# Filter features first, output sums in SBUF with 512-column products, and stores in a second DMA queue: a hybrid encoder layer

## The chip, the cores and the metric

One core of a Trainium2 chip runs the whole layer. The metric is the device time of one execution in microseconds (us); lower is better. Engines are named as in the profile: PE is TensorE (matmuls; PEld its weight loads), DVE is VectorE, ACT is ScalarE, POOL is GpSimd, SP is SyncE, which here only issues DMAs. HBM is the memory off the core, SBUF the memory on it, PSUM the banks that PE writes its sums to.

## What is computed

One layer, applied to two sequences of their own: p with 1024 tokens and s with 512, both of width 1024.

```
h = rmsnorm(x); z = h @ w_in                       # w_in is 1024 x 4096
x0, x1, vv = short_conv(first 3*512 columns of z)
y_hy  = x0 * long_conv(x1 * vv, hyena_filter(L))   # FFT convolution, filter from a small sine MLP
y_hy  = rmsnorm(y_hy) * silu(hy_gate)
q, k, v = att_qkv; q, k = rmsnorm(q), rmsnorm(k)   # 8 heads of 64
y_att = rmsnorm(neighbourhood_attention(q, k, v)) * silu(att_gate)
out = x + concat(y_hy, y_att) @ w_out              # w_out is 1024 x 1024
hyena_filter: h = sin(fr1*(z@w1 + b1)); h = sin(fr2*(h@w2 + b2)); h @ w3, times a decay
```

## The kernel before

Every large product is split into a high and a low part of each factor (`hi`, `lo`, type fp32r) and takes three matmuls: hi·hi, lo·hi, hi·lo. The weights come as 128x1024 tiles (`wraw`); ACT or DVE rounds each half to `whi` (line 364), POOL subtracts to get `wlo` (line 365), and `take_w` hands them out in the order of a list that `plan` has written ahead (lines 320 to 330).

The work is a sequence of stages. In each, `weave` (line 332) alternates between generators by a table of spans and priorities (`run`, lines 1133 to 1139), and a scheduler then sets the order of the instructions on each engine.

1. **Opening** (lines 1164 to 1173). The x tiles of p are loaded, squared on ACT, scaled on DVE by a reciprocal root (`x_norm`, `rsqrt`: 15 small DVE instructions), transposed on PE, and split into `hThi_p` (ACT) and `hTlo_p` (DVE) (`x_turn`), in two halves (segments) of 512 tokens. Then come the filter features (`filters_mlp`, line 155): two layers, three segments of 512 columns (two of p, one of s), each with one matmul, seven DVE instructions on `arg` and `n` and a sine on ACT.
2. **Filters** (`k_phase`): the filters times the decay (`dec`), their transforms stored to HBM (`K_d`), woven with the projections for q, k, v and gates of p, which are stored to HBM too (`qk_d`, `v_d`, `ga_d`). The tile `vg` of the v projection has one buffer: ACT writes its high part, DVE its low part, four DMAs store it, and only then comes the next.
3. **hyena_p**: convolutions of p, results to HBM (`A_d`).
4. **Attention of p with hyena and projections of s.**
5. **Output with attention of s.** `out_part(part, jobs)`: part 0 multiplies the hyena half, part 1 the attention half. The jobs are three blocks of 512 tokens: p first half (P0), p second half (P1), s. The order is part 0 of P0 and P1, part 1 of both, part 0 of s, and after the attention of s part 1 of s. A product is 128 tokens by 256 columns; two of them fill one PSUM bank. The sums of P0 and s stay in SBUF (`acc`, which starts as x). Those of P1 go through HBM: ACT scales the bank to `oo` (line 1106), `sum<-oo` stores it, and later `oy<-sum` and `ox` are loaded, added on POOL and finished on DVE.

All DMAs, loads and stores alike, are issued by SP in one in-order queue (`dma`, line 58):

```
def dma(self, out, in_):
    eng = (self.nc.sync, self.nc.scalar)[0]
    eng.dma_start(out=out, in_=in_)
```

Of the kernel before, what the change touches and what calls it, by code (L numbers as in the profile page):

```python
# [38 lines left out]
class Group:  # L39
    def __init__(self, name, L, x, out, z2, dec, tw0):  # L40
        self.name, self.L, self.x, self.out, self.z2, self.dec = name, L, x, out, z2, dec
        self.nt = L // P
# [4 lines left out]
        self.nseg = L // 512


class Kernel:  # L50
# [49 lines left out]
    def setup(self):  # L100
# [48 lines left out]
    def mlp_load(self):  # L149
        for w, nm in zip(self.w12, ("w1", "w2")):  # L150
            self.dma(w, self.io[nm])
        for G in (self.P_, self.S_):
            self.dma(self.z[G.name], G.z2)

    def filters_mlp(self, G, mp):
        nc = self.nc
        w1, w2 = self.w12
        h = self.z[G.name]
        for layer, (w, b, fr) in enumerate(((w1, "b1", "fr1"), (w2, "b2", "fr2"))):
            nxt = None if layer else mp.tile([P, G.L], F32, name=f"h1_{G.name}")  # L160
            for s in range(G.nseg):
                sl = slice(s * 512, (s + 1) * 512)
                ps = self.bank("ml")
                nc.tensor.matmul(ps, lhsT=w, rhs=h[:, sl], start=True, stop=True)
                arg = mp.tile([P, 512], F32, name="arg", bufs=2)
                self.ts(arg, ps, self.v[b], ALU.add, self.v[fr], ALU.mult)
                n = mp.tile([P, 512], F32, name="n", bufs=2)
                magic = 12582912.0
                self.ts(n, arg, 1.0 / TWO_PI, ALU.mult, magic, ALU.add)
                self.ts(n, n, magic, ALU.subtract)  # L170
                c1 = 6.28125
                c2 = 0.0019350051879882812
                c3 = TWO_PI - c1 - c2
                self.stt(arg, n, -c1, arg)
                self.stt(arg, n, -c2, arg)
                self.stt(arg, n, -c3, arg)
                self.ts(arg, arg, 3.1415925, ALU.min, -3.1415925, ALU.max)
                nc.scalar.activation(out=nxt[:, sl] if nxt else arg, in_=arg, func=AF.Sin)
                if layer:
                    self.stack([t[:, sl] for t in self.hm[G.name]], arg)  # L180
            h = nxt
            yield
# [35 lines left out]
    def x_norm(self, G, xp, ahead):  # L218

        nc = self.nc  # L220
        G.xs = []
        for s in range(G.nseg):
            ss = xp.tile([P, 4], F32, name="ss", bufs=2)
            for j in range(4):
                tt = s * 4 + j
                x = xp.tile([P, D], F32, name="x", bufs=G.nt)
                self.dma(x, G.x[tt * P:(tt + 1) * P, :])
                sq = xp.tile([P, D], F32, name="xsq", bufs=1)
                nc.scalar.activation(out=sq, in_=x, func=AF.Square, accum_out=ss[:, j:j + 1])
                G.xs.append(x)  # L230
                if ahead:
                    ahead.pop(0)()
            r = self.rsqrt(xp, ss, 4, 1.0 / D, "x")
            for j in range(4):
                x = G.xs[s * 4 + j]
                self.ts(x, x, r[:, j:j + 1])

    def x_turn(self, G, hps):

        nc = self.nc  # L240
        G.hi = [p.tile([P, KC, 512], F32R, name=f"hThi_{G.name}") for p in hps]
        G.lo = [p.tile([P, KC, 512], F32R, name=f"hTlo_{G.name}") for p in hps]
        for s in range(G.nseg):
            for k in range(KC):
                ps = self.bank()
                for j in range(4):
                    nc.tensor.transpose(out=ps[:, j * P:(j + 1) * P], in_=G.xs[s * 4 + j][:, k * P:(k + 1) * P], identity=self.ident)
                gk = self.v["norm_g"][:, k:k + 1]
                nc.scalar.activation(out=G.hi[s][:, k], in_=ps, func=AF.Copy, scale=gk)
                self.stt(G.lo[s][:, k], ps, gk, f32(G.hi[s][:, k]), ALU.subtract)  # L250
# [43 lines left out]
    def steps(self, what):  # L294
# [1090 lines left out]
```

## Time and profile before

| | |
|---|---|
| median of 3 runs | 1091.8 us (1089.95 to 1094.8) |
| the profiled execution: time, span | 1090.92 us, 1089.1 us |
| PE, DVE, ACT, POOL busy | 92%, 73%, 43%, 38% |
| granted TensorE clock, mean | 0.982 |
| DMA: one queue of program transfers | 153.69 MB |

The span runs from the first to the last instruction. The profiled execution lies 0.9 us under the median. PE's busy share counts modelled ends of pipelined matmuls, and time at the lower clock as busy, so it overstates what PE achieved.

### The profile page before, as it was taken

The numbers are of one execution on the slowest core, as the hardware profiler recorded it, in microseconds if no ns is written. First come the engines' busy times: TensorE is split into PE (matmuls) and PEld (weight loads), VectorE is DVE, ScalarE is ACT, GpSimd is POOL, SyncE is SP. The second block draws the span as 40 slices with busy tenths as digits, with TensorE's granted clock in tenths as the row PEclk, the third lists the DMA queues.
The fourth block names the chain that finished last, engine by engine and source line by source line (L and its number), as shares of the span: only waits on it lengthen the run. The fifth ranks groups of instructions, "written<-read, shape, count | busy, mean of one in ns | idle before, by whom it ended". The sixth has DMA issues, their size and how long they took to land.

```text
span 1089.1 us, 18072 instructions
## 1 busy us (share of the span) xinstructions
PE 1003.6 (92%) x6444; PEld 906.6 (83%) x6444; DVE 800.1 (73%) x2134; ACT 463.1 (43%) x958; POOL 415.5 (38%) x336
## 2 busy tenths in 40 slices
PE   3898999988999999999989999987989989899997
PEld 2698999977788888888877887876968879899987
DVE  5997779552157767967559999887967977587874
ACT  6453334233331323122124565655747653476530
POOL 2032332112142323123256344354254356784651
PEclk9999999999999999999989999999999999999999
DMA  8226372756312121212483354435544478966522
GB/s 299 69 78 195 119 235 91 242 161 241 109 39 80 58 62 58 67 54 92 173 240 106 94 145 130 129 100 168 141 133 115 132 237 263 295 183 211 173 72 97
DMA packets 112216, 154.84 MB, mean 142 GB/s; under 512 B 7953, under 2 KB 80475, under 8 KB 111615
## 3 DMA queue, kind: packets, MB, share of 16 engines
q1 hardware_dynamic: 112127, 153.69, 45.3%
q8 instruction: 51, 0.84, 0.3%
q14 instruction: 38, 0.31, 0.1%
HBM read 110.35 MB, written 43.32 MB: 141 GB/s over the span
## 4 chain that ended last, share of the span: by engine, by line
PE 48%; DVE 27%; DMA 12%; issue 5%; ACT 4%; SPq 2%; POOL 1%; POOLq 0%; DVEq 0%; ACTq 0%
PE bank L391 25%; PE bank L1094 7%; PE bank L443 3%; PE bank L404 3%; DMA dec<-in_dec_p_dram 2%; PE bank L1012 2%; SPq L60 2%; DVE zc L63 2%; DMA v_p<-vg 2%; DMA v_s<-vg 2%; PE bank L445 2%; PE bank L444 2%; DVE s_sb L981 2%; PE bank L1003 2%; DVE s L63 1%
## 5 line engine op out<-in xcount | busy, mean ns | idle before, releaser
L365 POOL TENSOR_TENSOR wlo<-wraw,whi 128x512 fp32r<-128x512 f32 x160 | 233.7, 1464 | 514.3 <-ACT whi L364 322.5
L391 PE MATMUL bank<-hThi_p,whi 128*128 128x512 f32 x320 | 126.8, 396 | 3.9 <-DVE vg L63 3.2
L391 PE MATMUL bank<-hThi_p,wlo 128*128 128x512 f32 x320 | 126.7, 396 | 0.0
L391 PE MATMUL bank<-hTlo_p,whi 128*128 128x512 f32 x320 | 126.3, 395 | 0.0
L404 PE MATMUL bank<-whi,hThi_p 128*128 128x256 f32 x384 | 111.6, 293 | 6.3 <-DVE vg L63 3.2
L1094 PE MATMUL bank<-whi,hi 128*128 128x256 f32 x384 | 111.6, 292 | 6.0 <-ACT oo L1106 2.6
L1094 PE MATMUL bank<-whi,lo 128*128 128x256 f32 x384 | 110.7, 292 | 0.9 <-POOL lo L63 0.9
L1094 PE MATMUL bank<-wlo,hi 128*128 128x256 f32 x384 | 110.9, 290 | 0.0
L404 PE MATMUL bank<-wlo,hThi_p 128*128 128x256 f32 x384 | 110.6, 289 | 0.0
L404 PE MATMUL bank<-whi,hTlo_p 128*128 128x256 f32 x384 | 108.4, 287 | 0.0
L985 ACT ACTIVATE s_sb<-s_sb,mx 128x360 f32<-128x360 f32 (+1 forms) x96 | 60.3, 629 | 88.2 <-DVE mx L981 87.8
L364 ACT CAST whi<-wraw 128x512 fp32r<-128x512 f32 x66 | 40.9, 623 | 108.0 <-PE bank L391 72.9
L1094 PEld LDWEIGHTS bank<-whi,hi 128*128 128x128 f32 x384 | 75.4, 196 | 7.4 <-ACT oo L1106 2.8
L404 PEld LDWEIGHTS bank<-whi,hThi_p 128*128 128x128 f32 x384 | 74.2, 194 | 8.2 <-DVE vg L63 3.7
L364 DVE CAST whi<-wraw 128x512 fp32r<-128x512 f32 x94 | 58.6, 626 | 27.6 <-POOL lo L63 6.8
L1094 PEld LDWEIGHTS bank<-whi,lo 128*128 128x128 f32 x384 | 74.6, 196 | 1.6 <-POOL lo L63 1.6
L404 PEld LDWEIGHTS bank<-wlo,hThi_p 128*128 128x128 f32 x384 | 74.5, 194 | 1.0 <-issue 1.0
L1094 PEld LDWEIGHTS bank<-wlo,hi 128*128 128x128 f32 x384 | 75.2, 196 | 0.0
L391 PEld LDWEIGHTS bank<-hThi_p,whi 128*128 128x128 f32 x320 | 60.4, 189 | 17.1 <-DVE vg L63 4.1
L404 PEld LDWEIGHTS bank<-whi,hTlo_p 128*128 128x128 f32 x384 | 73.3, 193 | 0.3 <-issue 0.2
L391 PE MATMUL bank<-hThi_s,whi 128*128 128x512 f32 x160 | 65.6, 413 | 8.4 <-DVE vg L63 4.9
L1012 PE MATMUL bank<-pt,V 120*64 120x256 f32 (+1 forms) x352 | 66.5, 295 | 6.6 <-DVE pt L63 4.2
(279 smaller groups left out, 2765.8 us busy)
## 6 DMA issues: line engine op xcount, KB each, us to landing
wraw<-in_w_ch_dram SPq DMA_DIRECT2D x40, 512.0 KB
wraw<-in_w_tk_dram SPq DMA_DIRECT2D x24, 512.0 KB
wraw<-in_w_out_dram SPq DMA_DIRECT2D x16, 512.0 KB
V<-v_p SPq DMA_DIRECT2D x32, 240.0 KB
v_p<-vg SPq DMA_DIRECT2D x32, 160.0 KB
K_p<-Kw SPq DMA_DIRECT2D x4, 1088.0 KB
x<-in_x_prompt_dram SPq DMA_DIRECT2D x8, 512.0 KB
dec<-in_dec_p_dram SPq DMA_DIRECT2D x16, 256.0 KB
```

The costliest lines, as they stand in the source:

```text
L60: eng.dma_start(out=out, in_=in_)
L63: (eng or self.nc.vector).tensor_tensor(out=out, in0=a, in1=b, op=op)
L364: next(self.w_round)(out=hi, in_=r)
L365: nc.gpsimd.tensor_tensor(out=lo, in0=r, in1=f32(hi), op=ALU.subtract)
L391: nc.tensor.matmul(ps, lhsT=w, rhs=h[s][:, k], start=(k == 0 and i == 0), stop=(k == KC - 1 and i == 2))
L404: nc.tensor.matmul(pss[t // 2][:, t % 2, :], lhsT=h[t // 4][:, k, t % 4 * P:(t % 4 + 1) * P], rhs=w, start=(k == 0 and i == 0 and t % 2 == ...
L443: mm(o, lhsT=c, rhs=z, start=True, stop=False)
L444: mm(o[:, 0:P], lhsT=ns if inverse else s, rhs=z[:, 1], start=False, stop=False)
L445: mm(o[:, P:], lhsT=s if inverse else ns, rhs=z[:, 0], start=False, stop=True)
L985: nc.scalar.activation(out=s_sb[:, :n], in_=s_sb[:, :n], func=AF.Exp, bias=mx, scale=-1.0, accum_out=l)
L1012: nc.tensor.matmul(o, lhsT=vl, rhs=pr_, start=(c == 0 and i == 0), stop=(c == ncu - 1 and i == 1))
L1094: nc.tensor.matmul(ps[:, j, :], lhsT=h[:, tok], rhs=w, start=(k == 0 and i == 0 and j == 0), stop=(k == 3 and i == 2 and j == 1))
```

## The change

The feature layer of the filters is cut into single segments (`mlp_seg`). The first segment of p, with its loads, comes ahead of x, and a hand-set order on DVE covers the opening: segment 0 of layer one, both halves of x, then the rest. One step of the argument reduction is dropped (three multiply-adds become two), and a Newton step of `rsqrt` takes three DVE instructions in place of four. The first two `wlo` are made on DVE. In the output all three jobs keep their sums in SBUF, each product has 512 columns and fills a bank by itself, part 0 runs for all three jobs at once (so w_out is loaded 12 times 512 KB and not 16), and `sum`, `oo`, `oy` and `ox` are gone. All stores are issued by ACT (`store`).

```diff
+    def store(self, out, in_):
+        self.nc.scalar.dma_start(out=out, in_=in_)
...
+        self.w_low = itertools.chain([nc.vector] * 2, itertools.repeat(nc.gpsimd))
...
-    def filters_mlp(self, G, mp):
...
+    def mlp_seg(self, G, mp, layer, s):
...
+        ps = self.bank("ml")
+        nc.tensor.matmul(ps, lhsT=w, rhs=h[:, sl], start=True, stop=True)
+        arg = mp.tile([P, 512], F32, name="arg", bufs=2)
+        self.ts(arg, ps, b, ALU.add, fr, ALU.mult)
+        n = mp.tile([P, 512], F32, name="n", bufs=2)
+        magic = 12582912.0
+        self.ts(n, arg, 1.0 / TWO_PI, ALU.mult, magic, ALU.add)
+        self.ts(n, n, magic, ALU.subtract)
+        c1 = 6.28125
+        self.stt(arg, n, -c1, arg)
+        self.stt(arg, n, c1 - TWO_PI, arg)
+        self.ts(arg, arg, 3.1415925, ALU.min, -3.1415925, ALU.max)
+        nc.scalar.activation(out=arg if layer else self.h1[G.name][:, sl], in_=arg, func=AF.Sin)
...
             self.mul(t, y, y)
-            self.mul(t, t, h)
-            self.ts(t, t, -0.5, ALU.mult, 1.5, ALU.add)
-            self.mul(y, y, t)
+            self.stt(t, t, -0.5, h, ALU.mult)
+            self.stt(y, t, 1.5, y, ALU.mult, ALU.add)
...
-            return [[]] + [[("w_out", g, int(what[3]))] for g in range(4)]
+            n = {"out0": 3, "out1": 2, "out1s": 1}[what]
+            return [[]] + [[("w_out", h, int(what[3]), u) for u in range(2)] if j == 0 else [] for h in range(2) for j in range(n)]
...
-            nc.gpsimd.tensor_tensor(out=lo, in0=r, in1=f32(hi), op=ALU.subtract)
+            self.sub(lo, r, f32(hi), next(self.w_low))
...
-        self.dma(self.K_d[G.name][blk], K)
+        self.store(self.K_d[G.name][blk], K)
...
+        for h in range(2):
+            hs = slice(h * 512, (h + 1) * 512)
+            units = [self.take_w(("w_out", h, part, k // 2)) for k in range(4)]
             for jb in jobs:
...
+                if part == 0:
+                    self.dma(acc[:, :, hs], G.x[t0 * P:(t0 + 4) * P, hs].rearrange("(t p) c -> p t c", p=P))
+                for t in range(4):
+                    ps = self.bank(next(self.mm_tags))
+                    tok = slice(t * P, (t + 1) * P)
+                    for k, (whi, wlo) in enumerate(units):
+                        hi, lo = jb["hi"][k][:, tok], jb["lo"][k][:, tok]
+                        for i, (w, a) in enumerate(((whi, hi), (wlo, hi), (whi, lo))):
+                            nc.tensor.matmul(ps, lhsT=a, rhs=w, start=(k == 0 and i == 0), stop=(k == 3 and i == 2))
+                    o = acc[:, t, hs]
+                    self.stt(o, ps, r[:, t0 + t:t0 + t + 1], o)
                     if part == 1:
-                        self.dma(rows(G.out), o)
+                        self.store(G.out[(t0 + t) * P:(t0 + t + 1) * P, hs], o)
...
-            [(["out0", "out1", "out0"], (0.0, 0.97), 0), (["att_s"], (0.0, 0.9), 4000)],
-            [(["out1"], every, 0)],
+            [(["out0", "out1"], (0.0, 0.97), 0), (["att_s"], (0.0, 0.9), 4000)],
+            [(["out1s"], every, 0)],
...
+        with self.tc.high_priority(4000), self.tc.manual_schedule(engines={self.nc.vector.engine}):
+            self.mlp_load(Gp)
+            self.mlp_seg(Gp, mp, 0, 0)
+            self.x_norm(Gp, 0, xp)
+            self.issue_w()
+            self.x_turn(Gp, 0, hp0)
+            self.x_norm(Gp, 1, xp)
+            self.issue_w()
+            self.x_turn(Gp, 1, hp1)
+            self.mlp_load(Gs)
+            self.mlp_seg(Gp, mp, 0, 1)
+            self.mlp_seg(Gs, mp, 0, 0)
+        for G, sg in ((Gp, 0), (Gp, 1), (Gs, 0)):
+            self.mlp_seg(G, mp, 1, sg)
...
-        self.weave(self.chain(self.out_part(0, jobs[:2]), self.then(more_w), self.out_part(1, jobs[:2]), self.out_part(0, jobs[2:])),
-                   self.attention(Gs, ap))
+        self.w_pools, self.w_bufs = itertools.cycle((wp, self.wp)), 8
+        self.weave(self.chain(self.out_part(0, jobs), self.out_part(1, jobs[:2])), self.attention(Gs, ap))
         self.weave(self.out_part(1, jobs[2:]))
```

The same replacement of `dma` by `store` is made for all results that go to HBM: `hT_d`, `qk_d`, `v_d`, `ga_d`, `A_d` and the two outputs. By the built program ACT gets 136 stores; SP keeps 348 of 502 DMAs.

The first place where the order moves is DVE in the opening, around the scaling of the second half of x (`x<-x,rs_y`; `arg` and `n` belong to the filter features, `rs_` to the reciprocal root, `dftm` to transform tables). Before:

```order
L63 TENSOR_TENSOR rs_y_250<-rs_y_250,rs_t_251 128x4
L75 SCALAR_TENSOR_TENSOR arg<-n,arg 128x512
L63 TENSOR_TENSOR rs_t_251<-rs_y_250 128x4
L81 TENSOR_SCALAR arg<-arg 128x512
L81 TENSOR_SCALAR arg<-bank,pc 128x512
L63 TENSOR_TENSOR rs_t_251<-rs_t_251,rs_h_249 128x4
L81 TENSOR_SCALAR n<-arg 128x512
L81 TENSOR_SCALAR rs_t_251<-rs_t_251 128x4
L79 TENSOR_SCALAR n<-n 128x512
L63 TENSOR_TENSOR rs_y_250<-rs_y_250,rs_t_251 128x4
L75 SCALAR_TENSOR_TENSOR arg<-n,arg 128x512
L79 TENSOR_SCALAR x<-x,rs_y_250 128x1024 x4
```

With the change:

```order
L79 SCALAR_TENSOR_TENSOR rs_t_312<-rs_t_312,rs_h_310 128x4
L79 SCALAR_TENSOR_TENSOR rs_y_311<-rs_t_312,rs_y_311 128x4
L67 TENSOR_TENSOR dftm<-km_505 128x256
L67 TENSOR_TENSOR rs_t_312<-rs_y_311 128x4
L79 SCALAR_TENSOR_TENSOR rs_t_312<-rs_t_312,rs_h_310 128x4
L79 SCALAR_TENSOR_TENSOR rs_y_311<-rs_t_312,rs_y_311 128x4
L83 TENSOR_SCALAR x<-x,rs_y_311 128x1024 x4
L79 SCALAR_TENSOR_TENSOR hTlo_p<-bank,pc,hThi_p 128x512 x8
L85 TENSOR_SCALAR arg<-bank,pc 128x512
```

Before, 18 instructions of the filter features stand between the first and the second scaling of x; now none does, and all but six of the features' instructions follow the second half's `hTlo_p`. The six (segment 0, layer one) stand at the head of DVE's order.

The second place is ACT in the fourth stage, at the v projection of s (`vg`); `s_sb`, `pt` and `ya` belong to the attention of p, `W` and `cgh` to the hyena of s. Before:

```order
L845 CAST vg<-bank 128x8x64
L985 ACTIVATE s_sb,l<-s_sb,mx 128x480
L1022 ACTIVATE qkr<-ya 128x512
L637 COPY W<-bank 128x256
L1005 CAST pt_5626<-bank 120x4x128
L985 ACTIVATE s_sb,l<-s_sb,mx 128x360
```

With the change:

```order
L855 CAST vg<-bank 128x8x64
L1015 CAST pt_5589<-bank 120x3x128
L1015 CAST pt_5589<-bank 120x4x128
L64 DMA v_s_121<-vg 40x2x512 x2
L995 ACTIVATE s_sb,l<-s_sb,mx 128x360
L647 COPY W<-bank 128x256
L1026 COPY ya<-bank 64x8x32
L64 DMA v_s_122<-vg 40x2x512
L995 ACTIVATE s_sb,l<-s_sb,mx 128x480
L64 DMA v_s_122<-vg 40x2x512
L1001 ACTIVATE s_sb<-s_sb,rl 128x360
L855 CAST vg<-bank 128x8x64
```

ACT now has the four stores between its own work. The first waits until DVE has made the low part of `vg`, and the exponentials and copies behind it on ACT wait with it; the next `vg` comes when the four have landed.

## Rows read from the trace of the kernel before

**Rows 1.** The page: busy time by engine, and the chain that ended last by engine

```profile
PE 1003.6 (92%) x6444; PEld 906.6 (83%) x6444; DVE 800.1 (73%) x2134; ACT 463.1 (43%) x958; POOL 415.5 (38%) x336
...
PE 48%; DVE 27%; DMA 12%; issue 5%; ACT 4%; SPq 2%; POOL 1%; POOLq 0%; DVEq 0%; ACTq 0%
```

**Rows 2.** Five stretches: start:end, us; busy of PE, PEld, DVE, ACT, POOL; clock, DMA

```profile
0.00:18.00 18.00, 0.00 (x0) 0.00 (x0) 7.41 (x17) 11.81 (x20) 5.68 (x11) 1.00 0.90 329
18.00:44.00 26.00, 21.28 (x136) 17.83 (x136) 23.56 (x56) 12.95 (x24) 0.00 (x0) 0.98 0.45 157
...
550.00:890.00 340.00, 309.46 (x1919) 273.59 (x1919) 288.73 (x731) 192.93 (x394) 150.22 (x130) 0.97 0.48 136
890.00:960.00 70.00, 64.32 (x495) 63.60 (x494) 45.01 (x106) 31.59 (x68) 52.15 (x51) 0.93 0.92 287
960.00:1062.00 102.00, 98.62 (x801) 96.70 (x800) 83.82 (x208) 54.88 (x129) 62.14 (x56) 1.00 0.51 154
```

**Rows 3.** The timeline of the opening, DVE: start, us, instruction

```profile
10.89 1.22 DVE L63 TENSOR_TENSOR rs_t<-rs_t,rs_h 128x4 f32<-128x4 f32 x1
...
16.41 0.16 DVE L63 TENSOR_TENSOR rs_t<-rs_y 128x4 f32<-128x4 f32 x1
...
31.39 0.80 DVE L81 TENSOR_SCALAR arg<-bank,pc 128x512 f32<-128x512 f32 x1
...
33.19 0.42 DVE L81 TENSOR_SCALAR n<-arg 128x512 f32<-128x512 f32 x1
...
34.19 0.68 DVE L75 SCALAR_TENSOR_TENSOR arg<-n,arg 128x512 f32<-128x512 f32 x1
...
44.19 2.74 DVE L79 TENSOR_SCALAR x<-x,rs_y 128x1024 f32<-128x1024 f32 x4
```

**Rows 4.** The same timeline, SP, PE and ACT

```profile
10.11 0.31 SPq L60 DMA_DIRECT2D z_p<-in_z_p_dram  x1
...
18.10 2.80 PE L247 MATMUL bank<-ident,x 128*128 128x128 f32 x12 [18.10 <-DVE x L79]
...
39.85 1.28 ACT L178 ACT_TABLE_LOAD   x1
...
41.15 1.15 ACT L178 ACTIVATE h_p<-arg 128x512 f32<-128x512 f32 x2
...
42.67 2.07 PE L164 MATMUL bank<-h_p,w 128*128 128x512 f32 x2 [4.21 <-DVE arg L81]
```

**Rows 5.** The chain of waits: start, us, what; matmuls in unbroken runs

```profile
280.71 33.17 PE bank L391 x145
...
747.84 8.16 DMA v_s<-vg
...
906.70 11.02 PE bank L1094 x91
```

**Rows 6.** Groups by line: count, busy us and mean ns, idle before

```profile
L63 DVE TENSOR_TENSOR xk<-bank,dec 128x512 f32<-128x512 f32 x24 | 16.4, 687 | 18.8 <-DMA dec<-in_dec_p_dram 9.1 <-DMA dec<-in_dec_s_dram 7.0 <-PE bank L553 1.6
...
L81 DVE TENSOR_SCALAR rs_t<-rs_t 128x4 f32<-128x4 f32 (+4 forms) x54 | 12.3, 230 | 1.1
...
L63 POOL TENSOR_TENSOR oy<-oy,ox 128x512 f32<-128x512 f32 x8 | 10.9, 1365 | 8.5 <-DMA oy<-sum 8.5
...
L1106 ACT ACTIVATE oo<-bank,rh_p 128x256 f32<-128x256 f32 x16 | 6.6, 470 | 21.0 <-PE bank L1094 14.0 <-DMA sum<-oo 6.6 <-DMA qkr<-q_s 0.3
```

**Rows 7.** Waits of SP's queue: for whom, us in total, times, longest

```profile
SPq L60 <- DVE vg L63: 40.4, 10, 9.6
...
SPq L60 <- POOL raw L63: 23.9, 6, 9.6
```

**Rows 8.** The tile vg: its store DMAs (ns min/median/max), and waits (us, times)

```profile
L60 SPq DMA_DIRECT2D v_p<-vg x32: 273/374/1291, 206.8 to 275.0; - x32
...
  DMA v_p<-vg: 18.3, 5
  DMA v_s<-vg: 16.5, 3
```

More of the change, by code (lines that the diff above doesn't have):

```diff
@@ L147, in mlp_setup, with mlp_load @@
             self.z[G.name] = mp.tile([66, G.L], F32, name=f"z_{G.name}")
[L149 to L152, printed above, removed]
+    def mlp_load(self, *gs):
+        for G in gs:
             self.dma(self.z[G.name], G.z2)
-    def filters_mlp(self, G, mp):
+            for w, nm in zip(self.w12, ("w1", "w2")) if G is self.P_ else ():
+                self.dma(w, self.io[nm])
+            self.h1[G.name] = None
@@ L156, in filters_mlp @@
+    def mlp_seg(self, G, mp, layer, s):
         nc = self.nc
[L157 to L182, printed above, removed]
@@ new lines, in mlp_seg @@
+        w, b, fr = self.w12[layer], self.v[f"b{layer + 1}"], self.v[f"fr{layer + 1}"]
+        sl = slice(s * 512, (s + 1) * 512)
+        if not layer and not s:
+            self.h1[G.name] = mp.tile([P, G.L], F32, name=f"h1_{G.name}")
+        h = self.h1[G.name] if layer else self.z[G.name]
+        ps = self.bank("ml")
+        nc.tensor.matmul(ps, lhsT=w, rhs=h[:, sl], start=True, stop=True)
+        arg = mp.tile([P, 512], F32, name="arg", bufs=2)
+        self.ts(arg, ps, b, ALU.add, fr, ALU.mult)
@@ new lines, in mlp_seg @@
+        n = mp.tile([P, 512], F32, name="n", bufs=2)
[7 more added lines that the diff above has]
+        nc.scalar.activation(out=arg if layer else self.h1[G.name][:, sl], in_=arg, func=AF.Sin)
+        if layer:
+            self.stack([t[:, sl] for t in self.hm[G.name]], arg)
@@ L211, in rsqrt, with x_norm @@
             self.mul(t, y, y)
-            self.mul(t, t, h)
-            self.ts(t, t, -0.5, ALU.mult, 1.5, ALU.add)
-            self.mul(y, y, t)
+            self.stt(t, t, -0.5, h, ALU.mult)
+            self.stt(y, t, 1.5, y, ALU.mult, ALU.add)
         return y
-    def x_norm(self, G, xp, ahead):
+    def x_norm(self, G, s, xp):
         nc = self.nc
-        G.xs = []
-        for s in range(G.nseg):
-            ss = xp.tile([P, 4], F32, name="ss", bufs=2)
-            for j in range(4):
[L225 to L250, printed above, removed]
+        ss = xp.tile([P, 4], F32, name="ss", bufs=2)
@@ new lines, in x_norm @@
+        xs = []
+        for j in range(4):
+            tt = s * 4 + j
+            x = xp.tile([P, D], F32, name="x", bufs=G.nt)
+            self.dma(x, G.x[tt * P:(tt + 1) * P, :])
+            sq = xp.tile([P, D], F32, name="xsq", bufs=1)
+            nc.scalar.activation(out=sq, in_=x, func=AF.Square, accum_out=ss[:, j:j + 1])
+            xs.append(x)
+        if not s:
+            self.fetch_w()
+        r = self.rsqrt(xp, ss, 4, 1.0 / D, "x")
+        for j in range(4):
+            self.ts(xs[j], xs[j], r[:, j:j + 1])
@@ new lines, in x_norm, with x_turn @@
+        G.xs += xs
+    def x_turn(self, G, s, hp):
+        nc = self.nc
+        hi = hp.tile([P, KC, 512], F32R, name=f"hThi_{G.name}")
+        lo = hp.tile([P, KC, 512], F32R, name=f"hTlo_{G.name}")
+        G.hi.append(hi)
+        G.lo.append(lo)
+        for k in range(KC):
+            ps = self.bank()
+            for j in range(4):
+                nc.tensor.transpose(out=ps[:, j * P:(j + 1) * P], in_=G.xs[s * 4 + j][:, k * P:(k + 1) * P], identity=self.ident)
+            gk = self.v["norm_g"][:, k:k + 1]
+            nc.scalar.activation(out=hi[:, k], in_=ps, func=AF.Copy, scale=gk)
+            self.stt(lo[:, k], ps, gk, f32(hi[:, k]), ALU.subtract)
@@ L341, in weave, with load_w @@
             assert end == (left[i] == 0), (i, left[i], end)
+    def load_w(self, raw, key):
+        if key[0] != "w_out":
+            self.dma(raw, self.io[key[0]][key[1:]])
+            return
+        _, h, part, u = key
+        for g in range(2):
+            self.dma(raw.rearrange("p (k g c) -> p k g c", k=2, g=2)[:, :, g],
+                     self.io["w_out"][h * 2 + g, part].rearrange("p (k c) -> p k c", k=4)[:, u * 2:u * 2 + 2])
     def fetch_w(self):
@@ L349, in fetch_w @@
             raw = pool.tile([P, 1024], F32, name="wraw", bufs=2)
[L350 removed]
+            self.load_w(raw, key)
             self.w_raw.append((key, raw, pool))
@@ L784, in tail @@
             self.stt(x0, x0, v["on_hy"][:, blk:blk + 1], gh, ALU.mult)
-            self.dma(self.A_d[G.name][blk], x0)
+            self.store(self.A_d[G.name][blk], x0)
             yield
@@ L832, in qk_proj @@
                     self.mul(o, o, r[:, m * 8:(m + 1) * 8].rearrange("p (n o) -> p n o", o=1).broadcast_to([P, 8, HD]), nc.gpsimd)
-                self.dma(self.qk_d[G.name][nm, gi].rearrange("(t p) c -> p t c", p=P), raw)
+                self.store(self.qk_d[G.name][nm, gi].rearrange("(t p) c -> p t c", p=P), raw)
                 yield
@@ L1074, in out_part @@
                 self.sub(lo, a, f32(hi), nc.gpsimd)
-            if part == 0 and "accs" in jb:
+            if part == 0:
                 jb["acc"] = jb["accs"].tile([P, 4, D], F32, name="acc")
         yield
-        for g in range(4):
-            gs = slice(g * 256, (g + 1) * 256)
-            units = [[t.rearrange("p (k c) -> p k c", c=256) for t in self.take_w(("w_out", g, part))] for _ in range(2)]
+        for h in range(2):
+            hs = slice(h * 512, (h + 1) * 512)
+            units = [self.take_w(("w_out", h, part, k // 2)) for k in range(4)]
@@ L1081, in out_part @@
             for jb in jobs:
[L1082 to L1084 removed]
+                G, t0, acc = jb["G"], jb["seg"] * 4, jb["acc"]
                 r = G.ratt if part else G.rhy
[L1086 to L1116 removed]
@@ L1219, in run @@
         cms, pools = [], {}
-        for n in ("ops0", "ops1", "acc0", "first", "last", "ops2", "acc2"):
+        for n in ("ops0", "ops1", "acc0", "acc1", "ops2", "acc2"):
             c, pools[n] = opn(n, "right")
```

60 lines of the change are left out of this document (10 added, 50 removed).

## The prediction

> **What bounds the kernel now.** I read the page first: PE is busy 92% of the span, and the chain that ended last passes through PE for 48%, DVE for 27% and DMA for 12%, but through ACT for 4% only [rows 1]. So the time is PE's work plus the stretches in which PE stands still, and those I looked for with busy times by stretch [rows 2]. The first 18 us hold no matmul. From 18 to 44 us PE is busy 21.28 of 26, DVE 23.56: DVE leads. From 550 to 890 us (attention of p with projections of s) PE loses 30.5 of 340, with DVE busy 288.73 and ACT 192.93. The output loses 5.7 from 890 to 960 us, at a DMA share of 0.92, and 3.4 from 960 to 1062 us. In the opening's timeline the reader is to see two things. Some reciprocal-root instructions took 1.22 us where a like one took 0.16, and the second scaling of x starts only at 44.19 us [rows 3]; PE had stood 4.21 us before 42.67, waiting for DVE's `arg` [rows 4].
>
> The sums below are against the profiled execution, 1090.9 us; it lies 0.9 under the median, which I add at the end. A difference under 0.5% (5.5 us: between 1086.3 and 1097.3) is about what a measurement of this kernel can't tell from none.
>
> **Opening: -6.4.** Added ahead of the first scaling: the loads of `z_p`, `w1`, `w2` at 0.31 us of SP's issue each, 0.9, and, before the fourth square on ACT, a table load and a sine, 1.28 + 0.58 [rows 4]; that makes +2.8. Removed: four root instructions ran while POOL subtracted `wlo`, at about 1.06 more than the 0.16 of a quiet one; with the first two `wlo` on DVE, after the scaling, these 4.2 go, and three dropped instructions at 0.16 give 0.5 [rows 3]. So -1.9. The six feature instructions at DVE's head stand where DVE waits for x and cost nothing as long as `z_p` arrives before x; if it comes as late as the last x tile, they cost their own 3.4. PE's other loss here, 18.00 to 44.00 us, is 4.7 [rows 2]. Ahead of the second scaling 18 feature instructions go: three at 0.80, eight at 0.42, seven at 0.68, together 10.5; two `wlo` at about the 0.68 of an instruction of 512 columns come, +1.4 [rows 3]. So that scaling comes 1.9 + 9.1 = 11 us earlier, at about 33, before PE has run out of first-half products (it did shortly before 38.5). I take PE's whole 4.7, less 0.2 for its restart: -1.9 - 4.5 = -6.4. The ends are -11, if all that DVE gains were time, and +1, if the loads and the sine hold up x and the features, now late, hold the stage behind.
>
> **Products of 512 columns: -7.7.** The output has 3 jobs x 2 parts x 4 x 4 x 4 x 3 = 1152 products of 256 columns; 91 in an unbroken run took 11.02 us, 121.1 ns each, so 139.5. It will have 576 of 512; 145 such in the projections took 33.17 us, 228.8 ns each, so 131.8 [rows 5]. The ends are 0 and -7.7, 0 where the attention of s sets the pace. The Trainium skill (TensorE: Matmul & The Clock Gate, section "Wait — 56ns, not 53.3ns?") has matmuls start columns ÷ 2.4 GHz plus some 2.5 ns apart; by it halving the count saves an estimated 576 x 2.5 ns = 1.5 us, and the whole sum would be 6.2 higher. The two measured spacings differ from that rule, and I go by them.
>
> **Other work of the output: -2.** The second half of p loses its way through HBM: 16 `oo` on ACT (470 ns, 21.0 us of waits before them) and 8 POOL additions (1365 ns, 8.5 us waiting for `sum`) [rows 6], 4 MB of sums stored and loaded again, and four w_out loads of 512 KB. All of this lies beside PE's work; what it can free is PE's idle, 9.1 us from 890 to 1062 [rows 2]. Against it, part 0 for three jobs loads 1 MB of `A` more at the stage's start, 3.7 us at the 287 GB/s of that stretch, where DMA is full. I take -2; the ends are -9.1 and +3.7. DVE finishes 48 products of twice the columns instead of 80, taken at nothing.
>
> **Shorter reciprocal roots: -2.** One of four instructions per Newton step goes, 54 in all at 230 ns [rows 6], 12.4 us of DVE; 17 stand in the attention of p, 3.9 us, where DVE is busy 85% [rows 2]. Half of it is taken, since PE waits there for other things too; the ends are 0 and -4.
>
> **Stores out of SP's queue: -2.** SP waited 40.4 us for the low part of `vg` and 23.9 for POOL's `raw` before it could issue their stores [rows 7], and loads queued behind. These waits leave SP. The stores of v then need no turn behind loads; DVE and ACT together waited 18.3 and 16.5 us for them to land before the one buffer of `vg` came free [rows 8], and one such store is 8.16 us of the chain [rows 5]. I take a quarter of that 8.16; the ends are 0 and -8. The Trainium skill (DMA: Bandwidth & Descriptors, section "Issuing engines are not separate DMA queues") says that transfers issued by several engines share the same 16 DMA engines, so that only issue time is spared. By it this term is an estimated 0 and the sum 2 higher; the trace of before, with one issuing queue, can't show it.
>
> **Stores in ACT's order: +5.** This is the wait that the change adds. ACT issues 136 stores; at 0.37 us, a store's median on SP [rows 8], that is 50 us of its time. It also takes over SP's two waits, 64.3 us in 16 times, 4.0 each [rows 7]. Behind a waiting store stand ACT's exponentials, copies out of PSUM and `whi` roundings, and for those wait DVE and PE. The chain passes through ACT for 4% [rows 1]; 4% of 64.3 + 50 is 4.6, and I take 5. Below, 0: ACT is free 147 of 340 us in the attention of p [rows 2], and the scheduler put other ACT work between `vg` and its stores. Above, half of the 64.3, 32, as SP too waited while DVE and POOL did other work.
>
> The sum: -6.4 - 7.7 - 2 - 2 - 2 + 5 = -15.1, 1075.8 us; with the 0.9, 1076.7, say **1077**.
>
> **Rivals.**
> *The stores hold ACT* (slower). In the attention of p, ACT waits at the stores of `vg` for DVE's low part, DVE waits for ACT's exponentials behind them, and PE starves. For it: four stores per `vg` and an in-order engine between two busy ones. Against: ACT's small share of the chain. At half of the 64.3 us the time is 1091.8 - 20.1 + 32 = 1104. It beats the gains from 20.1 us on, and is measurably slower from 25.6.
> *The opening gives back its gain.* The k phase waits for the features, which now come last on DVE, and for `dec` (18.8 us of DVE's idle before `xk`, most of it for that load [rows 6]). Then PE gains 1 instead of 6.4: 1082.
> *The attention of s sets the output.* Then 7.7 + 2 bring nothing: 1086.4, on the edge of measurable. For it: DVE 83.82 of 102 us. Against: PE 98.62 of 102 [rows 2].
> *Stores in a queue of their own bring more.* They land without loads ahead (-8), ACT's free time takes their issue (+1), and the opening gives 11: 1091.8 - 11 - 7.7 - 2 - 2 - 8 + 1 = 1062.
> *The sums or the wider products don't come about*: the program has 576 products of 512 columns, so this has no chance worth a number.
>
> **How the numbers follow.** My forecast (1068 to 1085 by itself) gets 0.46, the stores holding ACT 0.13, the opening giving back 0.12, the attention of s 0.09, the quick stores 0.13; 0.07 goes to a middle case in which ACT costs 15 to 25 us and nothing measurable is left. Faster: 0.46 + 0.12 + 0.13 and half of 0.09, less a little for the upper edge, 0.75; same: 0.07 and the other half, 0.12; slower 0.13. For 8 in 10 the range must take in the quick stores at nearly their full size, 1060, and at the top the attention of s and the middle case, 1095; it leaves out the worst of the first rival.
>
> **What would show it.** The second scaling of x near 33 us and no 4 us of idle PE before 42; output products near 229 ns in a stage some 8 to 10 us shorter; the idle of PE in the attention of p, 30.5 us, within 5 of what it was; ACT's stores a small share of the chain. Wrong would be: a chain that goes through ACT's queue for more than 2% of the span, PE's idle up by 15 us in the attention of p, or a k phase that starts no earlier though x does.

## The result, and the profile after

The changed kernel took 1098.4 us (median of 7 runs, 1096.37 to 1102.4), the kernel before 1092.2 beside it: ratio 1.0062, 95% interval [1.0033, 1.0091]. It is slower by 6.8 us, where I forecast 15 us less. Below, "us against before" is a ratio's distance from 1 times 1092.2.

On the page of the changed kernel PE's busy time stayed (1003.6 before [rows 1]), and the chain's share of ACT went from 4% to 6%, that of ACT's queue (ACTq) from 0% to 1%:

```profile
PE 1004.6 (92%) x5868; PEld 876.0 (80%) x5868; DVE 786.2 (72%) x2036; ACT 454.7 (41%) x942; POOL 393.2 (36%) x318
...
PE 50%; DVE 25%; DMA 11%; ACT 6%; issue 5%; POOL 1%; ACTq 1%; SPq 1%; DVEq 0%; POOLq 0%
```

Busy times of the changed kernel by stretch, columns as in [rows 2]; the last two are the attention of p as a stage (from the first matmul of hyena's sum of squares to the last of its output transposes, which bounds every row of this kind below) and the rest of the program:

```profile
0.00:18.00 18.00, 4.12 (x4) 1.00 (x4) 6.59 (x17) 11.34 (x19) 2.59 (x9) 1.00 0.84 315
18.00:44.00 26.00, 21.28 (x150) 19.18 (x151) 22.24 (x47) 14.21 (x29) 0.66 (x1) 1.00 0.51 166
...
549.80:901.50 351.70, 319.28 (x1948) 279.31 (x1946) 293.12 (x720) 195.68 (x399) 156.91 (x134) 0.97 0.48 140
901.50:1096.50 195.00, 175.21 (x865) 144.82 (x864) 129.37 (x295) 78.10 (x175) 88.89 (x86) 0.95 0.48 151
```

The same two of the kernel before:

```profile
548.90:893.90 345.00, 314.46 (x1953) 278.59 (x1952) 293.37 (x736) 194.01 (x397) 153.97 (x131) 0.97 0.49 140
893.90:1089.10 195.20, 180.17 (x1437) 176.51 (x1435) 136.57 (x342) 86.11 (x194) 114.80 (x105) 0.98 0.62 189
```

So 0.9 us are lost before the attention of p, where 6.4 less were forecast, and 6.7 in it; the output stage gained 0.2 where 9.7 were forecast. DVE is equally busy in the attention of p (293 us): what differs is how long it stands still, 58.6 us after 51.6 (the row's length less DVE's busy time).

In the opening of the changed kernel (timeline) the fourth square of x waits on ACT behind a table load and the sine, so the root starts at 14.55 and the first transposes at 19.82, not 18.10 [rows 4]; POOL still made two `wlo`, and two root instructions still took over 1.1 us. The second scaling came at 38.61 and not 44.19 [rows 3]:

```profile
11.55 1.28 ACT L180 ACT_TABLE_LOAD   x1
...
12.85 0.63 ACT L180 ACTIVATE h_p<-arg 128x512 f32<-128x512 f32 x1
...
13.38 1.04 ACT L227 ACTIVATE xsq<-x 128x1024 f32<-128x1024 f32 x1
...
14.55 0.17 DVE L85 TENSOR_SCALAR rs_h<-ss 128x4 f32<-128x4 f32 x1 [3.92 <-ACT xsq L227]
...
16.34 1.12 DVE L67 TENSOR_TENSOR rs_t<-rs_y 128x4 f32<-128x4 f32 x1
...
19.82 2.80 PE L246 MATMUL bank<-ident,x 128*128 128x128 f32 x12 [9.90 <-DVE x L83]
...
38.61 2.74 DVE L83 TENSOR_SCALAR x<-x,rs_y 128x1024 f32<-128x1024 f32 x4
```

The lead is gone by the end of the k phase. Its first and its last products, and the first transposes of the convolutions of p behind it (grouped by line: count, ns, first and last start), of the kernel before:

```profile
L553 PE MATMUL bank<-w3lof,hm_p x16: 282/283/283, 61.0 to 138.5; 128*128 128x256 f32 x16
...
L553 PE MATMUL bank<-w3lob,hm_s x8: 283/283/283, 193.3 to 224.8; 128*128 128x256 f32 x8
...
L612 PE MATMUL bank<-ident,cx x48: 270/272/328, 313.7 to 831.6; 128*128 128x128 f32 x48
```

and of the changed kernel:

```profile
L563 PE MATMUL bank<-w3lof,hm_p x16: 281/283/283, 72.7 to 145.5; 128*128 128x256 f32 x16
...
L563 PE MATMUL bank<-w3lob,hm_s x8: 280/283/283, 208.9 to 245.4; 128*128 128x256 f32 x8
...
L622 PE MATMUL bank<-ident,cx x48: 270/273/328, 315.7 to 842.8; 128*128 128x128 f32 x48
```

### The profile page after: what moved, and what is told of

Read it like the earlier page. It is cut to its first block, busy times and chain, and to the rows that moved or that the text cites. A ratio compares the mean times of both kernels' runs of the same rounds, so it can differ in the third digit from the quotient of the medians.

```text
span 1096.5 us, 16729 instructions
## 1 busy us (share of the span) xinstructions
PE 1004.6 (92%) x5868; PEld 876.0 (80%) x5868; DVE 786.2 (72%) x2036; ACT 454.7 (41%) x942; POOL 393.2 (36%) x318
## 4 chain that ended last, share of the span: by engine, by line
PE 50%; DVE 25%; DMA 11%; ACT 6%; issue 5%; POOL 1%; ACTq 1%; SPq 1%; DVEq 0%; POOLq 0%
PE bank L401 27%; PE bank L1101 7%; PE bank L453 3%; PE bank L414 2%; DMA dec<-in_dec_p_dram 2%; PE bank L1022 2%; DVE whi L374 2%; DMA v_p<-vg 2%; DVE s_sb L991 2%; PE bank L455 1%; PE bank L454 1%; PE bank L1013 1%; DVE s L67 1%; DMA hT<-px 1%; DVE pt L67 1%
## 5 line engine op out<-in xcount | busy, mean ns | idle before, releaser
L67 POOL TENSOR_TENSOR wlo<-wraw,whi 128x512 fp32r<-128x512 f32 x150 | 222.0, 1486 | 510.6 <-ACT whi L374 283.0
L1101 PE MATMUL bank<-whi,hi 128*128 128x512 f32 x192 | 78.0, 408 | 6.1 <-ACT hi L1082 4.0
L1101 PE MATMUL bank<-wlo,hi 128*128 128x512 f32 x192 | 76.9, 400 | 0.0
L1101 PE MATMUL bank<-whi,lo 128*128 128x512 f32 x192 | 76.4, 403 | 0.0
L1022 PE MATMUL bank<-pt,V 120*64 120x256 f32 (+1 forms) x352 | 69.5, 305 | 4.1 <-DVE pt L67 2.4
L401 PEld LDWEIGHTS bank<-hTlo_p,whi 128*128 128x128 f32 x320 | 60.4, 189 | 12.1
L401 PEld LDWEIGHTS bank<-hThi_p,wlo 128*128 128x128 f32 x320 | 60.6, 189 | 11.9
L374 DVE CAST whi<-wraw 128x512 fp32r<-128x512 f32 x86 | 52.3, 618 | 18.5 <-PE bank L401 5.0
L401 PE MATMUL bank<-hTlo_s,whi 128*128 128x512 f32 x160 | 65.4, 409 | 0.0
```

Source lines behind the costliest of these rows:

```text
L67: (eng or self.nc.vector).tensor_tensor(out=out, in0=a, in1=b, op=op)
L374: next(self.w_round)(out=hi, in_=r)
L401: nc.tensor.matmul(ps, lhsT=w, rhs=h[s][:, k], start=(k == 0 and i == 0), stop=(k == KC - 1 and i == 2))
L1022: nc.tensor.matmul(o, lhsT=vl, rhs=pr_, start=(c == 0 and i == 0), stop=(c == ncu - 1 and i == 1))
L1101: nc.tensor.matmul(ps, lhsT=a, rhs=w, start=(k == 0 and i == 0), stop=(k == 3 and i == 2))
```

## The experiments

All were timed against the kernel before in several rounds; "us" is the median of a run.

| run | kernel | us | ratio [95%] |
|---|---|---|---|
| e1 | changed, stores by SP | 1077.0 | 0.9864 [0.9842, 0.9886] |
| e2 | before, stores by ACT | 1095.6 | 1.0021 [1.0003, 1.0040] |
| e3 | before, opening changed | 1094.4 | 1.0041 [1.0019, 1.0063] |
| e4 | before, output changed | 1097.1 | 1.0037 [1.0014, 1.0060] |
| e5 | before, shorter roots | 1074.5 | 0.9821 [0.9792, 0.9850] |
| e6 | e1, one stage's stores by ACT | 1095.4 | 1.0026 [1.0006, 1.0047] |
| e7 | changed, raw and zero stores by SP | 1098.2 | 1.0034 [1.0011, 1.0056] |
| e8 | before, roots and output | 1070.3 | 0.9783 [0.9755, 0.9811] |
| e9 | before, v stores of s first | 1080.7 | 0.9894 [0.9865, 0.9923] |
| e10 | e7, ya stores by SP too | 1099.8 | 1.0070 [1.0047, 1.0095] |
| e11 | e8, all v stores first | 1071.9 | 0.9819 [0.9792, 0.9846] |
| e12 | e1, features ahead of x's second half | 1102.8 | 1.0096 [1.0073, 1.0119] |
| e13 | before, shorter roots up to the attention | 1083.9 | 0.9921 [0.9898, 0.9944] |
| e14 | e7, acc loads by ACT | 1081.6 | 0.9907 [0.9881, 0.9932] |
| e15 | e8, acc loads by ACT | 1082.7 | 0.9915 [0.9887, 0.9943] |
| e16 | e8, stores by ACT | 1095.6 | 1.0036 [1.0016, 1.0056] |

**Each part alone, and the stores taken back.** The edit of e1 follows; e2, e3, e4 and e5 apply one group of the diff's hunks to the kernel before (in e2 the sums kept in HBM stay on SP).

```diff
     def store(self, out, in_):
-        self.nc.scalar.dma_start(out=out, in_=in_)
+        self.nc.sync.dma_start(out=out, in_=in_)
```

> The changed kernel with its 136 stores issued by SP again; opening, roots and output as changed. Theory A, stores on ACT hold ACT's in-order work (the attention of p ended about 7 us later than before): about 7 us faster than the changed kernel, 1091, with the gain between 560 and 900 us. Theory B, the stores cost nothing and the loss is elsewhere: 1098. Theory C, ACT's queue lets stores land sooner and is a gain: slower than 1098.

> The kernel before with one thing changed: its results (all but the sums kept in HBM) are stored through ACT. Theory A: 1092 + 7 = 1099. Theory B: 1092. Theory C: 1088 or less. My prediction's sum has +5 for ACT and -2 for sooner landing, so 1095.

> The kernel before with the changed opening alone (feature segments, order on DVE, first two low weight parts on DVE; roots, output and stores as before). Prediction's term: -6.4, so 1086. Rival D, the k phase waits for features that now come later, and the gain is given back there: 1091 to 1094, with the transposes of the second half ending some 7 us earlier and the first inverse-filter products some 8 us later than in the kernel before.

> The kernel before with the changed output alone (products of 512 columns, all sums in SBUF, w_out loaded 12 times). Prediction's terms: -7.7 - 2, so 1082. Rival E, the attention of s sets the end of the output stage whatever PE's products take: 1090 to 1093, with the attention of s ending at the same time after its start (161 us) as before.

> The kernel before with the three-instruction Newton step alone. The version with stores on SP was 10 us shorter than before in the attention of p, though DVE was as busy there (292 us). Theory F, the shorter roots are worth that, through the waits in chains of tiny instructions and not through DVE's busy time: 1082, with the attention of p (first row sum to last column of A, 345 us before) at 335. Theory G, the gain needs the other parts as well, or comes from the order that the scheduler happened to write: 1088 to 1094. Prediction's term: -2, 1090.

e1 is 21.7 us faster than the changed kernel, three times what I expected; alone the stores cost 2.3 (e2). The opening costs 4.5 alone and the output 4.0: nearer to rivals D and E than to my terms, and a little above both. The roots gave 19.6, ten times my term. The attention of p in e1 and in e5:

```profile
550.20:883.90 333.70, 311.18 (x1940) 277.85 (x1940) 291.96 (x722) 194.81 (x400) 156.04 (x133) 0.97 0.50 147
```

```profile
541.60:874.30 332.70, 310.43 (x1951) 277.45 (x1950) 292.64 (x721) 194.33 (x399) 158.37 (x134) 0.97 0.51 148
```

With the long roots and stores on SP it takes 345, with the short ones 333, with the short ones and stores on ACT 352: ACT's stores cost the changed kernel, in this stage, 18 us, more than the 12 that the roots gave there. With the long roots and stores on ACT (e2) it takes 341.9:

```profile
554.20:896.10 341.90, 310.13 (x1942) 274.73 (x1941) 295.19 (x736) 197.83 (x401) 155.14 (x133) 0.98 0.48 142
```

So e2's 2.3 are a sum: in its profiled execution this stage is 3.1 us shorter than before, what lies ahead of it 5.3 longer and what lies behind it 4.5. The effects do not add: alone they sum to -8.8, together they are +6.8. One on top of the other, roots -19.6, output -4.1 (e8), opening +8.8 (e1), stores +21.7.

**What the roots did.** In e5 DVE's busy time in the attention of p fell by 0.7 us, the stage's length by 12.3. The chain of waits before holds two landings of v stores there, 8.16 [rows 5] and 9.24 us. In SP's timeline of the kernel before the load of the bias table stands ahead of the late fourth store:

```profile
745.72 1.41 SPq L60 DMA_DIRECT2D v_s<-vg  x3
747.22 0.57 SPq L60 DMA_DIRECT2D qkr<-in_rpb_dram  x1
747.84 0.53 SPq L60 DMA_DIRECT2D v_s<-vg  x1
```

With the short roots the scheduler had put all four together. e9 gives them a higher priority in the kernel before and shortens nothing; e13 leaves this order alone and shortens the roots ahead of it (`short` is false from the attention of p on).

```diff
+                        with self.tc.high_priority(20000 if G.name == "s" else 0):
+                            self.dma(dst[rr, :, m * 2:(m + 1) * 2, :], f32(vh[p0:p0 + 40]).rearrange("p t h d -> p t (h d)"))
```

```diff
             self.mul(t, y, y)
+            if self.short:
+                self.stt(t, t, -0.5, h, ALU.mult)
+                self.stt(y, t, 1.5, y, ALU.mult, ALU.add)
+                continue
```

> The kernel before with one order changed: on SP's queue the four stores of each v block of s stand together, where before the load of the bias table (in_rpb) stood ahead of the fourth one twice, and that store took 8.16 and 9.24 us to land. Nothing is shorter in it. Theory K, most of what the shorter roots gave in the attention of p (12 us) came from the order that they happened to bring, stores together and the table behind: 1092 - 8 to - 13, so 1080 to 1084. Theory F, the roots' own work gave it: 1092.

> The kernel before with the shorter roots up to the end of the convolutions of p alone; in the attention of p the long roots stay, and with them SP's order of before (the bias table ahead of the fourth v store of s, twice). Theory K: the attention of p keeps its 345 us, and the total is 1092 - 7 = 1085, the 7 us that the k phase gained with the shorter roots. Theory F, the roots are worth their gain in every stage by themselves: 1085 too, but only if the attention's 12 us come back with the long roots for another reason than the order; the run on the order alone (1081) speaks against it. If the k phase's 7 us were chance: 1092.

Theory K holds: e9's order alone gave 11.6 us, with the stage at 333.5 and DVE as busy as before. ACT's wait for the v stores to land, in that stage, fell from 13.8 us (first line, before) to 3.8 (second, e9; us, times, longest):

```profile
ACT vg L845 <- DMA v_s<-vg: 13.8, 2, 7.9
```

```profile
ACT vg L845 <- DMA v_s<-vg: 3.8, 2, 2.7
```

SP's timeline of e9, and its stage:

```profile
744.51 2.13 SPq L60 DMA_DIRECT2D v_s<-vg  x4
746.74 0.58 SPq L60 DMA_DIRECT2D qkr<-in_rpb_dram  x1
```

```profile
549.30:882.80 333.50, 309.73 (x1940) 274.95 (x1939) 293.02 (x734) 195.42 (x398) 154.47 (x132) 0.97 0.50 146
```

e13 gave 8.6, and its attention of p, with the table ahead of the fourth store again, stayed long:

```profile
542.60:885.60 343.00, 311.79 (x1954) 276.08 (x1953) 293.07 (x733) 194.40 (x398) 154.21 (x131) 0.98 0.49 142
```

So some 12 of the roots' 20 us are an order on SP's queue that came with them. Whether the other 8, ahead of the attention, are the shorter work or an order again stays open.

**Where ACT's stores cost.** e6 sets the stores of the attention of p alone on ACT; e7 takes those that wait for POOL (`raw`, zero rows of `v`) from ACT; e10 those of `ya` too (the last pair of lines); e16 is e8 with all on ACT.

```diff
-                self.store(self.qk_d[G.name][nm, gi].rearrange("(t p) c -> p t c", p=P), raw)
+                self.dma(self.qk_d[G.name][nm, gi].rearrange("(t p) c -> p t c", p=P), raw)
...
-                    self.store(self.v_d[G.name][gi][hf][320:360].rearrange("x h d -> x (h d)"), zt)
+                    self.dma(self.v_d[G.name][gi][hf][320:360].rearrange("x h d -> x (h d)"), zt)
...
-            self.store(self.A_d[G.name][4 + pr][:, sl], y)
+            self.dma(self.A_d[G.name][4 + pr][:, sl], y)
```

> The version with stores on SP (1077), but the stores of one stage, the attention of p with the projections of s, on ACT. Theory A in its narrower form, stores cost in the stage in which ACT and DVE feed each other: 1077 + 17 = 1094, and the attention of p takes 351 us and not 334. Rival H, the cost is spread over the stages: 1077 plus 5 to 9.

> The changed kernel with two kinds of stores back on SP, those that wait for POOL: raw (q and k) and the zero rows of v; all others stay on ACT. In the changed kernel ACT stood 7.0 us for raw and 8.2 for the zero tile in the attention of p. Theory I, these long waits of ACT make most of the cost: 1098 - 15 = 1083. Rival J, the cost lies in the issue time and the many short waits of all the other stores: 1094 to 1098.

> The changed kernel with the stores that wait for POOL (raw, zero rows of v) on SP, and those of the attention's result ya too; v, gates, filters, hyena results and outputs stay on ACT. In the run with the first two kinds on SP the attention of p took 322 us and not 351, but ACT then stood 19 us at the output's start, before its roundings of hi, until DVE had made ya for the store ahead of them; the attention of s began 44 us after the stage's start and not 18 to 26. Theory L, ACT's cost is these three kinds of store, each held by a late result: 1098 - 18 to - 24, so 1074 to 1080. Theory M, other stores on ACT cost the same elsewhere: 1090 or more.

> The version with shorter roots and the changed output (1070), all stores on ACT; the opening as before. Theory A: beside the short roots ACT's stores cost 18 to 21 us whatever the opening does, because the attention of p takes about 351 us and not 334: 1088 to 1091. Theory P: the cost of 21 belongs to the company of the changed opening as well; without it the stores cost what they did alone, 3: 1073.

e6 is as slow as before (+2.8), 17.7 us over e1; e16 is 27.6 over e8. Their attention of p takes 355.8 and 353.5 (e6 first):

```profile
549.80:905.60 355.80, 319.80 (x1948) 278.91 (x1946) 293.15 (x721) 195.98 (x400) 156.60 (x134) 0.97 0.47 140
```

```profile
547.00:900.50 353.50, 317.13 (x1948) 275.55 (x1947) 294.48 (x721) 196.25 (x400) 156.83 (x135) 0.98 0.47 139
```

So 17.7 of the 21.7 us lie in the stores of this one stage, and the cost doesn't need the changed opening. It comes in programs with the short roots and not in e2 with the long ones; no run has short roots and ACT's stores without the changed output. ACT's waits in that stage of the changed kernel (for whom, us, times, longest) name the stores fed by POOL, which I had not put in my first rival; a wait stands at the instruction behind the store:

```profile
ACT L995 <- POOL raw L67: 7.0, 1, 7.0
...
ACT s_sb L1001 <- POOL vg L864: 5.1, 1, 5.1
...
ACT L995 <- POOL vg L864: 3.1, 1, 3.1
```

Such waits come to 15.2 us here, 15.5 in e6 and 15.1 in e16; e1 has none, and e2 one of 2.9. Behind each of the three DVE stood still for ACT, 9.3 us together (DVE's timeline of the changed kernel):

```profile
590.43 0.16 DVE L997 RECIPROCAL rl<-l 128x1 f32<-128x1 f32 x1 [3.76 <-ACT s_sb L995]
...
780.84 0.16 DVE L997 RECIPROCAL rl<-l 128x1 f32<-128x1 f32 x1 [2.65 <-ACT s_sb L995]
...
822.63 0.75 DVE L79 SCALAR_TENSOR_TENSOR cvv<-bank,pc,cvv 128x511 f32<-128x511 f32 x1 [2.90 <-ACT cvv L424]
```

In the whole stage DVE stands still 58.6 us, in e1 41.7. So 9.3 of these 16.8 us are seen directly behind the POOL-fed stores; the rest may be their later effects or another order of the scheduler's, and no run parts the two. With these two kinds on SP (e7) the stage is 29 us shorter than in the changed kernel, but 10 of them are DVE work that stands elsewhere in e7 (282.76 us busy after 293.12), most of it behind the stage's end (136.57 after 129.37); DVE's standing fell by 19. The total gained nothing, since the output took 30 us more:

```profile
547.00:869.50 322.50, 304.11 (x1907) 271.33 (x1906) 282.76 (x717) 190.69 (x390) 146.80 (x125) 0.98 0.48 139
869.50:1094.80 225.30, 189.94 (x904) 156.26 (x904) 136.57 (x298) 84.01 (x185) 100.11 (x95) 0.91 0.46 150
```

Theory L fell with e10 (+7.6): without `ya` on ACT the output is as long. In both, SP's queue has acc's loads around the last load of `ga` and ahead of the first of the attention of s; SP's timeline of e7, and ACT's, where the rounding of `hi` stands behind the store of `ya`:

```profile
874.36 1.56 SPq L61 DMA_DIRECT2D acc<-in_x_prompt_dram  x3
876.66 2.53 SPq L61 DMA_DIRECT2D qkr<-ga_p  x1
...
888.06 0.94 SPq L61 DMA_DIRECT2D acc<-in_x_sample_dram  x2
...
892.78 0.38 SPq L61 DMA_DIRECT2D qkr<-k_s  x1
```

```profile
896.47 2.18 ACT L1082 CAST hi<-lo 128x512 fp32r<-128x512 f32 x4 [18.96 <-DVE ya L79]
```

**The loads of acc.** e14 and e15 issue the six loads of acc from ACT, in e7 and in e8.

```diff
-                    self.dma(acc[:, :, hs], G.x[t0 * P:(t0 + 4) * P, hs].rearrange("(t p) c -> p t c", p=P))
+                    self.nc.scalar.dma_start(out=acc[:, :, hs], in_=G.x[t0 * P:(t0 + 4) * P, hs].rearrange("(t p) c -> p t c", p=P))
```

> The changed kernel with the POOL-fed stores on SP (1098), and in it the six 1 MB loads of acc, which wait for nothing but free memory, issued by ACT. Theory N: there the gain of the attention of p was lost at the output's start because the last ga load, the last store of ya and the first loads of the attention of s stood behind acc's 1 MB loads in SP's queue; with these gone the attention of s begins 18 to 26 us after the stage's start and not 44, total 1074 to 1082. Rival O, the transfers share the DMA engines whichever engine issues them (share 1.02 there): it begins as late, 1094 or more.

> The version with shorter roots and the changed output (1070), its six 1 MB loads of acc issued by ACT. Theory N: the attention of s, which began 18 us after the stage's start, begins some 5 us earlier, 1064 to 1067. Rival O: 1070.

e14 came to the expected total (13.9 us under e7) but not by the expected way: by the trace the attention of s began 43 us after the stage's start, as late as in e7, and ran 15 us faster from there. In e15 the same edit cost 14 us. Which order of these loads is good depends on what else stands in the queues; why e14 gained stays open.

**The opening and the fastest version.**

> The kernel before with the shorter roots and the changed output; opening and stores as before. If the opening's order costs what it did alone (+2 to +4): 1073 to 1075, faster than the version with stores on SP at 1077. If the opening takes part in the gain (its order or the later k phase helps later stages): 1080 or more.

> The version with shorter roots and the changed output (1070), and in it the v stores of p and s ahead of other transfers in SP's queue. For s the order has the stores together already; for p the waits for v stores (24.9 us with the shorter roots alone, in a stretch of the k phase) may shrink. If those waits are on the path: 1064 to 1068; if not, or if K and dec come later for it: 1070 or more.

> The version with stores on SP (1077), but in the opening's order on DVE all remaining filter features come ahead of the second half of x. Theory D, the opening gave its gain back because the features came late, the k phase ended 20 us later and the convolutions of p waited for it: the k phase ends 10 us or more earlier than 246 us, and the convolutions start earlier than 316; total 1068 to 1074, if PE has first-half products enough meanwhile. Against D: the k phase ends earlier and the convolutions start no earlier, 1077 or more.

e8 is the fastest version, 23.7 us under before; against it the changed opening costs 8.8 (e1). e11, with v stores of p first too, is no better. e12 put the remaining features ahead of x's second half:

```diff
             self.x_turn(Gp, 0, hp0)
+            self.mlp_load(Gs)
+            self.mlp_seg(Gp, mp, 0, 1)
+            self.mlp_seg(Gs, mp, 0, 0)
+            for G, sg in ((Gp, 0), (Gp, 1), (Gs, 0)):
+                self.mlp_seg(G, mp, 1, sg)
             self.x_norm(Gp, 1, xp)
```

Its k phase ended 8 us earlier than e1's, but PE ran out of first-half products: 24 us idle in 60, at a granted clock of 0.74.

```profile
18.00:78.00 60.00, 35.67 (x214) 28.49 (x214) 47.10 (x87) 24.58 (x45) 2.02 (x2) 0.74 0.22 73
```

Its convolutions began at 334.9 us, 19 later than e1's, though its k phase ended earlier (238.1 and 245.8). So it can't tell whether late features alone delay the convolutions, and it shows that the k phase's end doesn't fix their start. Theory D is argued from e3 and the changed kernel's trace, and not shown.

## Why the prediction was wrong

*What bounds the kernel* held as far as PE's work goes; in the attention of p the loss shows in DVE's standing, 7.0 us more, and little in PE's, 32.4 us after 30.5. So two of my three signs of being wrong, PE's idle up by 15 and ACT's queue over 2% of the chain (it has 1%), would have missed it; the third came, the k phase starts at 72.7 us and not 61.0. The failure is in the sizes of the terms and in adding them.

- **Stores in ACT's order, +5**: the step that failed. On top of the other parts they cost 21.7 (e1), beyond the 20.1 from which my first rival decides. I weighed 114 us of waiting and issue with ACT's 4% of the chain before; the chain of before can't tell what a wait does that isn't there yet. The rival had the stage and the chain from ACT to DVE right, and named the wrong store: the long waits are not those of `vg` for DVE's low part but of `raw` and the zero rows for POOL; for `raw` [rows 7] showed them on SP, 23.9 us in 6 waits. That these waits are the cause is shown in part (9.3 us of DVE's standing behind them); the total of 21.7 is measured.
- **Shorter roots, -2**: -19.6 (e5). I priced 17 instructions of DVE. What came was the place of four stores against one load on SP's queue (e9, -11.6) and 8.6, mostly ahead of the attention (e13). The chain's row of 8.16 us [rows 5] was in my sum, put down to a turn behind loads in general; I did not look at which load.
- **Opening, -6.4**: +4.5 alone. The first scaling came 1.7 later and not 1.9 earlier: the root waited for a square that the sine held up. The second transposes came 5.6 earlier and not 11, and PE's idle from 18 to 44 us, which I took whole, stayed at 4.7 (21.28 of 26 busy in both kernels). The k phase, with the features last on DVE, ended 20.6 later, and the convolutions started 2.0 later. The gain was given back, as my second rival has it; that the late features are why is argued.
- **Products and other work of the output, -9.7**: +4.0 alone, -4.1 with short roots. A run of 70 products took 16.04 us, 229 ns each, as I took it, and PE's busy time in the stage fell by 5.0 us (180.17 to 175.21), but the attention of s sets the stage, my third rival: the last matmul of its sums of squares starts 167.7 us after the stage's start in both kernels (893.9 to 1061.6 before, first line; 901.5 to 1069.2 changed, second). Why the change alone costs 4.0 stays open.

```profile
L804 PE MATMUL bank<-ones,sqs x48: 168/250/271, 548.9 to 1061.6; 128*128 128x1 f32 x48
```

```profile
L814 PE MATMUL bank<-ones,sqs x48: 164/250/373, 549.8 to 1069.2; 128*128 128x1 f32 x48
```

The last 69 products, behind the attention of s, ran at 275 ns, at a granted clock of 0.81 in the last 27 us where the kernel before had 0.96:

```profile
911.34 16.04 PE bank L1101 x70
...
1073.56 18.99 PE bank L1101 x69
```

```profile
1064.80:1072.90 8.10, 1.87 (x8) 1.78 (x8) 4.58 (x16) 1.00 (x3) 1.26 (x1) 0.50 0.19 65
...
1069.60:1096.50 26.90, 18.97 (x69) 14.66 (x69) 8.12 (x22) 0.62 (x1) 1.27 (x1) 0.81 0.25 90
```

```profile
1054.90:1062.00 7.10, 6.14 (x50) 5.74 (x49) 4.84 (x7) 2.75 (x5) 5.97 (x5) 1.00 0.49 150
...
1061.90:1089.10 27.20, 21.23 (x168) 20.21 (x167) 11.42 (x33) 0.62 (x1) 3.61 (x3) 0.96 0.30 97
```

Between the two runs of products PE of the changed kernel was busy 1.87 us of 8.1, and the granted clock was 0.50, the lower level of 1.2 GHz; that of the kernel before had products left and kept the clock (first fence: changed kernel, second: before).

- **Stores out of SP's queue, -2**: alone with ACT's cost they are +2.3 (e2), so this gain isn't seen by itself. My two terms for the stores sum to +3, near that, but by luck: its stages don't show my terms, the attention of p, where I placed ACT's cost, is 3.1 shorter. The stores did go through a queue of their own, q10 on the page:

```profile
q1 hardware_dynamic: 77815, 106.17, 32.0%
q10 hardware_dynamic: 27880, 41.23, 10.9%
```

The Trainium skill (DMA: Bandwidth & Descriptors, section "Issuing engines are not separate DMA queues") says that these share the DMA engines and that only issue time is saved. The runs agree as far as totals go, no gain of the second queue shows (e2, +2.3). As e2's attention of p is shorter, a gain there isn't excluded. The place within one queue is worth 11.6 us (e9).

## What to carry to other kernels

Before moving stores to a compute engine, list for each what it waits for and who stands behind it there: a store fed by a third engine (here POOL) that comes late holds all that stands behind it. Taking such stores off ACT shortened the stage, but not the program (e7), so time the whole again. Where a scheduler writes the order, price an edit by the order it leaves on the DMA queue as well: look for a large load between the stores of a single-buffered tile, and pin the stores (e9; pinning those of p as well, e11, brought nothing). Gains read from one trace need not add: here the parts alone sum to -8.8 us and give +6.8 together.

## What was not expected of the hardware

A store of 160 KB with a bias table's load of 244 KB ahead of it in the same queue landed 8 to 9 us after its issue; with the store first, ACT's wait for such stores fell from 13.8 to 3.8 us (e9). And the granted clock in the tail went with the output's form: 0.81 in the changed kernel, 0.83 in e1, e4 and e8 over the 26 us from the last sum of squares, with 69 or 70 products of 512 columns. With 256 columns it was 0.91 to 0.99 in e3, e5 and e13, which have more left (168 to 198 products), and 0.88 and 0.89 in e2 and e9, which have as many columns left (138 and 139 products). What makes the difference was not tested.
